# A hybrid decoder layer on one core: the router's one-hots hold two ranks side by side, ids are divided once per four heads, and a spilled tile is asked for earlier

## The chip, the core and the metric

The kernel runs on one core of a Trainium2 chip. Time is device microseconds (us) of one execution of the whole program. The engines are called PE (TensorE, matrix multiplication), DVE (VectorE), ACT (ScalarE), POOL (GpSimd) and SP (SyncE, which here only starts transfers). Each engine takes its instructions strictly in its own order, and an instruction that waits holds back everything behind it on that engine.

## What is computed

One decoder layer for 512 tokens of width 1024, in float32: RMS norm, a projection, two recurrent branches (HGRN2 and retention) that are gated and merged, and then PEER, a mixer of 16384 tiny experts, of which each token uses 128. The part that matters here is PEER:

```python
s = jnp.einsum('thpd,hpkd->thpk', q, sub_keys)      # 8 heads, 2 halves, 128 keys
top_s, top_i = lax.top_k(s, 16)
cand = top_s[:, :, 0, :, None] + top_s[:, :, 1, None, :]
cand_idx = top_i[:, :, 0, :, None] * 128 + top_i[:, :, 1, None, :]
best_s, best_c = lax.top_k(cand.reshape(T, 8, 256), 16)
expert_idx = jnp.take_along_axis(cand_idx.reshape(T, 8, 256), best_c, axis=-1)
gates = jax.nn.softmax(best_s, axis=-1)
...
act = gelu(einsum('td,thkd->thk', x, expert_u[expert_idx]))
out = einsum('thk,thkd->td', gates * act, expert_v[expert_idx])
```

After it a residual sum and a final RMS norm give the output.

## The kernel before

A float32 product is made of three float32r matmuls: each operand is split into a high part, which ACT rounds (L76), and a low part, which DVE subtracts (L77); `mm3` (L89 to L92) multiplies low by high, high by high and high by low. Every 1 MB block of weights is loaded by SP into one of three `raw` buffers (L81), split by ACT and DVE into one of three `w` buffers, and used by PE; the third matmul of a group, L92 where the block stands on the left, is the one that needs DVE's low part.

The program runs in stages. Projections and the two branches come first (to about 856 us). Then come three stages that interleave two kinds of work. PE multiplies the first 384 tokens with all 16384 rows of expert_u and later of expert_v, since nearly every expert is used by some token; the last 128 tokens are done on DVE alone, from table rows that POOL gathers by index (`gather_step`, L674 to L689, four `row` buffers). The first 88 of 128 groups of 128 experts of expert_u are multiplied ahead (`u_ahead`, L698), between the router's and the gate stage's other work; their results go to DRAM (`spill`).

The **router** (L804 to L818) takes the eight heads one after the other. For a head, `route_keys` is PE's query projection; `route_top` (twice) finds the 16 best keys of each half on DVE; `route_pick` (L760 to L802), called Pick below, sums the candidates, finds the 16 best, and turns their positions into expert ids. For this it compares the positions with a table of 50 or 20 candidate numbers (`oh`, a one-hot in float16, L791), multiplies by the candidates' ids (`pr`, L794) and sums (`ef`, L795). The first 8 ranks need only 20 candidates, the last 8 need 50; four token tiles times 8 ranks make 640 and 1600 elements a row. Four small instructions (L798 to L801) divide an id into the two key numbers, and L802 writes those of the last 128 tokens to `e_last`, by which POOL gathers. Between these stand three blocks of expert_u per head, five at the last (`U_R`; a block holds two groups), and up to six gathered rows.

The **gate stage** (L862 to L890) makes, for 12 blocks of 32 tokens, a matrix of 128 x 128 gates a token: DVE builds float16 one-hots of eight tokens a step (`oa`, `ob`, L869, L870) and scales them (`og`), PE multiplies them (L881), ACT copies them to `stage` (L884), and ACT's queue writes `stage` to DRAM (`gd`, L890). `U_G` says after which of the steps a block is multiplied ahead.

The **V stage** (L900 on) multiplies the last 40 groups of expert_u (kind "new"), reads the spilled results back (kind "old", L955), multiplies by the gates (`gt`, read from `gd`, L906; L916), splits (w_hi, w_lo, L917) and multiplies with expert_v into six sums in PSUM (L928). At its first blocks PE's results lie in two PSUM buffers, which ACT empties (L635).

Then `finish` (L651 to L672) adds each tile's sum, normalises and writes out; of the four tiles the last 128 tokens come first, and tile 2 (`tt == DT - 1`) comes last. `rsqrt_mean` (L100 to L114) is the norms' helper: ACT's square root, DVE's reciprocal and one Newton step.

The order on each engine isn't the program's order. A scheduler places the instructions by their readiness in its own model and by priority; `fetch` (L601) gives the loads and splits of a block 30 places of priority (`PRIO`), so that they are placed ahead of work that the program has earlier. `order` (L584 to L598) lists the blocks: numbers 0 to 51 are multiplied ahead or belong to the router, and block 52 is the first of the V stage.

Of the kernel before, what the change touches and what calls it, by code (L numbers as in the profile page):

```python
# [20 lines left out]
D = 1024  # L21
# [23 lines left out]
U_R, U_G = ((2,) * 8, (1,) * 7 + (3,)), (0, 1, 0, 1, 0, 1, 0, 0)  # L45
GATHER_END = 4
PRIO = 30
G_SCALE = 2.0 ** 15
# [4 lines left out]
def block_kernel(ctx, tc, a, out):  # L53
# [46 lines left out]
    def rsqrt_mean(ss, k, n, name):  # L100

        v = small.tile([128, k], F32, name=name + "v", tag=f"rs_v{k}")
        DVE.tensor_scalar(v, ss, 1.0 / n, EPS, op0=OP.mult, op1=OP.add)
        s = small.tile([128, k], F32, name=name + "s", tag=f"rs_s{k}")
        ACT.activation(s, v, AF.Sqrt)
        r = small.tile([128, k], F32, name=name + "r", tag=f"rs_r{k}")
        DVE.reciprocal(r, s)
        t = small.tile([128, k], F32, name=name + "t", tag=f"rs_t{k}")
        DVE.tensor_tensor(t, r, r, op=OP.mult)
        DVE.tensor_tensor(t, t, v, op=OP.mult)  # L110
        DVE.tensor_scalar(t, t, -0.5, 1.5, op0=OP.mult, op1=OP.add)
        r2 = small.tile([128, k], F32, name=name + "q", tag=f"rs_q{k}")
        DVE.tensor_tensor(r2, r, t, op=OP.mult)
        return r2  # L114
# [486 lines left out]
    def fetch():  # L601
        if len(blocks) == len(order):
            return
        kind, pr = order[len(blocks)]
        with tc.high_priority(offset=PRIO):
            fetch_block(kind, pr)
# [44 lines left out]
    def finish(tt):  # L651
# [7 lines left out]
        for nb in range(2):  # L659
# [4 lines left out]
            ACT.activation(junk[:, n], d, AF.Square, accum_out=ss[:, nb:nb + 1])  # L664
        st = small.tile([128, 1], F32, name="fst", tag="ss1")
# [3 lines left out]
        for nb in range(2):  # L669
            n = slice(nb * 512, (nb + 1) * 512)  # L670
            DVE.scalar_tensor_tensor(res[:, n], acc[:, tt, n], r, wrow[:, n], op0=OP.mult, op1=OP.mult)
            nc.sync.dma_start(out[tt * 128:(tt + 1) * 128, n], res[:, n])  # L672
# [36 lines left out]
    with tc.tile_pool(name="rout", bufs=1, reuse_waits="tile") as ro:  # L709
# [8 lines left out]
        iotac = ro.tile([128, NCAND + NCAND8], F16, name="iotac")  # L718
        DVE.tensor_copy(iotac, iotaf)
        best = ro.tile([128, TT, PH, TOPK], F32, name="best")  # L720
        ids_a = ro.tile([128, TT, PH, TOPK], F32, name="ids_a")
# [38 lines left out]
        def route_pick(state, hd):  # L760
# [5 lines left out]
            def sums(dst, src, widths, offs):  # L766
                ones = sum(w == 1 for w in widths)
                n = len(widths) - ones
                lead = list(dst.shape[:-1])
                for i in range(n):  # L770
                    w = widths[i]
                    DVE.tensor_tensor(dst[..., offs[i]:offs[i] + w],
                                      src(0)[..., i:i + 1].to_broadcast(lead + [w]),
                                      src(1)[..., :w], op=OP.add)
                DVE.tensor_tensor(dst[..., offs[n]:offs[n] + ones], src(0)[..., n:n + ones],
                                  src(1)[..., 0:1].to_broadcast(lead + [ones]), op=OP.add)
# [8 lines left out]
            posh = ro.tile([128, TT, TOPK], F16, name="posh", tag="posh")  # L785
            DVE.tensor_copy(posh, pos)
            ef = ro.tile([128, TT, TOPK], F32, name="ef", tag="ef")
            for lo, n, io, ids in ((0, NCAND8, iotac[:, NCAND:], cid8), (8, NCAND, iotac[:, :NCAND], cand[:, 1])):
                shape = [128, TT, 8, n]
                oh = ro.tile(shape, F16, name="oh", tag=f"oh{n}")  # L790
                DVE.tensor_tensor(oh, io[:, None, None, :].to_broadcast(shape),  # L791
                                  posh[:, :, lo:lo + 8, None].to_broadcast(shape), op=OP.is_equal)
                pr = ro.tile(shape, F32, name="pr", tag=f"pr{n}")
                DVE.tensor_tensor(pr, oh, ids[:, :, None, :].to_broadcast(shape), op=OP.mult)  # L794
                DVE.tensor_reduce(ef[:, :, lo:lo + 8], pr, axis=X, op=OP.add)  # L795
            posf = ro.tile([128, TT, TOPK], F32, name="posf", tag="posf")
            af = ids_a[:, :, hd, :]
            DVE.tensor_scalar(posf, ef, 1.0 / NK, -63.5 / NK, op0=OP.mult, op1=OP.add)  # L798
            DVE.tensor_scalar(posf, posf, 12582912.0, None, op0=OP.add)
            DVE.tensor_scalar(af, posf, 12582912.0, None, op0=OP.subtract)  # L800
            DVE.scalar_tensor_tensor(ids_b[:, :, hd, :], af, -float(NK), ef, op0=OP.mult, op1=OP.add)  # L801
            DVE.tensor_copy(e_last[:, hd * TOPK:(hd + 1) * TOPK], ef[:, TT - 1, :])  # L802
# [97 lines left out]
    with tc.tile_pool(name="vp", bufs=2, reuse_waits="tile") as vp:  # L900
# [9 lines left out]
        def v_group(g, acts, gt, w_hi, w_lo):  # L910
            todo = []
            for pr in range(GE // 2):
                hi, lo = take("v", g * GE // 2 + pr)
                two = slice(2 * pr, 2 * pr + 2)
                w = acts[:, two, :].rearrange("p e (b t) -> p e b t", t=GT)
                DVE.tensor_tensor(w, w, gt[:, :, two, :].rearrange("p b e t -> p e b t"), op=OP.mult)  # L916
                split(w_hi[:, two, :], w_lo[:, two, :], acts[:, two, :])  # L917
# [26 lines left out]
        acts = {groups[0][1]: new_acts()}  # L944
        gates = {vs[0]: load_gates(vs[0])}
        for kind, g in groups:
            if kind != "v" and g not in acts:
# [6 lines left out]
            if kind == "old":  # L954
                nc.sync.dma_start(acts[g].rearrange("p e t -> p (e t)"), spill[g])  # L955
# [84 lines left out]
```

## Time and profile before

| what | us |
|---|---|
| median of three runs (2112.39 to 2117.42) | 2114.75 |
| the profiled execution | 2116.79 |
| its span, first to last instruction | 2115.0 |
| PE busy in the span | 2074.8 |
| DVE busy | 1501.1 |
| ACT busy | 809.0 |
| mean granted PE clock | 0.995 |

Times in the profile count from the span's start. Busy time of PE overlaps: a matmul starts before the one ahead of it has ended, so the sum of single durations is more than the time they took. An entry such as "PE mm L92 <- DVE w L77: 14.8, 9, 3.3" says that PE stood idle ahead of L92's matmuls for 14.8 us in 9 places, the longest 3.3 us, until DVE's L77 had written `w`. "L77 DVE ... x37 | 84.4, 2282" is a group of 37 instructions, busy 84.4 us in all, 2282 ns each.

### The profile page before, as it was taken

How to read it: one execution, taken by the hardware profiler on the slowest of the kernel's cores; microseconds unless marked ns; L12 is line 12 of the kernel's file. 1: busy time of each engine (PE TensorE's matmuls, PEld its weight loads, DVE VectorE, ACT ScalarE, POOL GpSimd, SP SyncE). 2: the span in 40 equal slices, each digit the busy share in tenths (PEclk: the TensorE clock that was granted, in tenths of full speed). 3: DMA queues.
4: the chain of work that ended last, by engine and by line, in shares of the span. 5: the costliest groups of instructions: out<-in, count | busy, mean ns of one | idle time of the engine just before them, and what ended most of it. 6: DMA issues, size and time to landing. Idle time of an engine off the chain costs nothing.

```text
span 2115.0 us, 27164 instructions
## 1 busy us (share of the span) xinstructions
PE 2074.8 (98%) x10635; PEld 1803.0 (85%) x10635; DVE 1501.1 (71%) x2847; ACT 809.0 (38%) x959; POOL 401.3 (19%) x271
## 2 busy tenths in 40 slices
PE   9999999999999999999989999999999999999998
PEld 6888888888888788899888999988888888888876
DVE  4677674454345445599899899987877887787776
ACT  4344342244233523333322377763323333233332
POOL 0000000000000000021311211123444443554450
PEclk9999999999999999999999999999999999999999
DMA  5212112322232232365565678899989999989993
GB/s 193 80 63 71 67 60 95 105 80 85 80 104 81 90 139 80 127 229 197 207 216 195 235 273 318 329 339 363 350 325 339 339 352 340 330 326 351 334 335 125
DMA packets 139490, 441.33 MB, mean 209 GB/s; under 512 B 9825, under 2 KB 59105, under 8 KB 120418
## 3 DMA queue, kind: packets, MB, share of 16 engines
q1 hardware_dynamic: 94288, 261.85, 35.6%
q0 software_dynamic: 37008, 135.28, 17.2%
q10 hardware_dynamic: 8066, 42.48, 5.2%
q8 instruction: 83, 1.36, 0.3%
q14 instruction: 45, 0.37, 0.0%
HBM read 395.00 MB, written 44.56 MB: 208 GB/s over the span
## 4 chain that ended last, share of the span: by engine, by line
PE 76%; DVE 13%; issue 4%; DMA 4%; ACT 2%; POOL 1%; SPq 0%; DVEq 0%; ACTq 0%; POOLq 0%
PE mm L90 16%; PE mm L92 16%; PE mm L91 16%; PE sum L92 7%; PE sum L90 7%; PE sum L91 7%; DVE w L77 3%; DMA row<-in_expert_v_dram,e_last 2%; DMA row<-in_expert_u_rows_dram,e_last 2%; PE aux L881 1%; PE aux L334 1%; DVE scr L727 1%; PE aux L376 1%; PE aux L470 1%; DVE idx L729 1%
## 5 line engine op out<-in xcount | busy, mean ns | idle before, releaser
L77 DVE TENSOR_TENSOR w<-raw,w 128x2048 fp32r<-128x2048 f32 x198 | 452.6, 2287 | 237.2 <-ACT w L76 236.5
L92 PE MATMUL mm<-h_hi,w 128*128 128x384 f32 (+1 forms) x1536 | 547.9, 357 | 17.0 <-DVE w L77 14.8
L90 PE MATMUL mm<-h_lo,w 128*128 128x384 f32 (+1 forms) x1536 | 551.0, 359 | 2.8 <-ACT acts L635 2.4
L91 PE MATMUL mm<-h_hi,w 128*128 128x384 f32 (+1 forms) x1536 | 547.8, 357 | 0.0
L76 ACT ACTIVATE w<-raw 128x2048 fp32r<-128x2048 f32 x198 | 378.8, 1913 | 416.6 <-PE mm L92 204.8
L92 PEld LDWEIGHTS mm<-h_hi,w 128*128 128x128 f32 x1536 | 291.4, 190 | 39.8 <-DVE w L77 17.9
L90 PEld LDWEIGHTS mm<-h_lo,w 128*128 128x128 f32 x1536 | 291.5, 190 | 23.2 <-ACT acts L635 2.7
L91 PEld LDWEIGHTS mm<-h_hi,w 128*128 128x128 f32 x1536 | 291.5, 190 | 19.3
L90 PE MATMUL sum<-w,w_hi 128*128 128x512 f32 x768 | 299.0, 389 | 2.5 <-DVE w L77 2.5
L92 PE MATMUL sum<-w,w_lo 128*128 128x512 f32 x768 | 299.0, 389 | 1.7 <-DVE w_lo L77 1.7
L91 PE MATMUL sum<-w,w_hi 128*128 128x512 f32 x768 | 298.9, 389 | 0.0
L645 POOL DMA_INDIRECT row<-in_expert_u_rows_dram,e_last x128 | 181.1, 1414 | 566.6 <-DVE junk L679 340.9
L645 POOL DMA_INDIRECT row<-in_expert_v_dram,e_last x128 | 216.8, 1694 | 241.3 <-DVE acc L686 213.6
L686 DVE SCALAR_TENSOR_TENSOR acc<-row,dots,acc 128x1024 f32<-128x1024 f32 x128 | 164.0, 1281 | 35.3 <-DMA row<-in_expert_v_dram,e_last 33.7
L679 DVE SCALAR_TENSOR_TENSOR junk<-row,h_last 128x1024 f32<-128x1024 f32 x128 | 156.3, 1221 | 34.2 <-DMA row<-in_expert_u_rows_dram,e_last 33.5
L90 PEld LDWEIGHTS sum<-w,w_hi 128*128 128x128 f32 x768 | 144.2, 188 | 33.0 <-DVE w L77 3.4
L92 PEld LDWEIGHTS sum<-w,w_lo 128*128 128x128 f32 x768 | 144.2, 188 | 32.0 <-DVE w_lo L77 2.1
L91 PEld LDWEIGHTS sum<-w,w_hi 128*128 128x128 f32 x768 | 144.2, 188 | 29.7
L711 POOL DMA_DIRECT2D keys<-in_keys_dram x1 | 0.7, 714 | 859.6 <-DVE acc L571 859.6
L90 PE MATMUL mm<-w,h_hi 128*128 128x512 f32 x384 | 151.2, 394 | 0.0
L92 PE MATMUL mm<-w,h_lo 128*128 128x512 f32 x384 | 150.4, 392 | 0.0
L91 PE MATMUL mm<-w,h_hi 128*128 128x512 f32 x384 | 150.4, 392 | 0.0
(270 smaller groups left out, 2455.8 us busy)
## 6 DMA issues: line engine op xcount, KB each, us to landing
raw<-in_expert_u_dram SPq DMA_DIRECT2D x64, 1024.0 KB
raw<-in_expert_v_dram SPq DMA_DIRECT2D x64, 1024.0 KB
gd<-stage ACTq DMA_DIRECT2D x12, 2048.0 KB
gt<-gd SPq DMA_DIRECT2D x32, 768.0 KB
spill<-actw ACTq DMA_DIRECT2D x44, 384.0 KB
acts<-spill SPq DMA_DIRECT2D x22, 768.0 KB
raw<-in_w_rv_dram SPq DMA_DIRECT2D x8, 1024.0 KB
raw<-in_w_rg_dram SPq DMA_DIRECT2D x8, 1024.0 KB
```

The costliest lines, as they stand in the source:

```text
L76: ACT.activation(hi, src, AF.Copy)
L77: DVE.tensor_tensor(lo, src, hi.bitcast(F32), op=OP.subtract)
L90: PE.matmul(ps, lhi, rlo, start=first, stop=False)
L91: PE.matmul(ps, lhi, rhi, start=False, stop=False)
L92: PE.matmul(ps, llo, rhi, start=False, stop=last)
L334: PE.matmul(ps[:, c * 192:(c + 1) * 192], k[:, (c0 + c) * 128:(c0 + c + 1) * 128], mv[:, c0 + c, :, :].rearrange("p v t -> p (v t)"), star ...
L376: PE.matmul(po[:, j * 128:(j + 1) * 128], amat(i, j), v[:, i, hd * 128:(hd + 1) * 128], start=(i == 0), stop=(i == j))
L470: PE.matmul(ps[:, :w], k[e][:, i * 128:(i + 1) * 128], q[e][:, i * 128:], start=(e == 0), stop=(e == 1))
L645: POOL.indirect_dma_start(out=r, out_offset=None, in_=src, in_offset=bass.IndirectOffsetOnAxis(ap=e_last[:, i:i + 1], axis=0))
L679: tc.keep_in_program_order(DVE.scalar_tensor_tensor(junk, r, 1.0, h_last, op0=OP.mult, op1=OP.mult, accum_out=dots[:, i:i + 1]))
L686: tc.keep_in_program_order(DVE.scalar_tensor_tensor(x_last, r, dots[:, i - 128:i - 127], x_last, op0=OP.mult, op1=OP.add))
L727: DVE.match_replace(scratch, vals[:, 0:8], src, -3e38)
```

## The change

**Pick.** The table of candidate numbers holds each number twice, and `oh` gets the shape [16, n, 2]: two neighbouring ranks lie side by side in the last dimension, so every operand of the comparison has step 1 there. The product and the sum are made for each of the two ranks by itself, so two instructions become four (twice), of half the size. The ids stay in a tile for all heads, and the division into key numbers is done after heads 3 and 7, for four heads at a time. In `sums`, candidate rows of equal width go into one instruction, which takes one instruction of 16 elements off each head.

**Priorities and places.** `U_G` spaces the blocks of the gate stage otherwise. Block 0 gets 180 places of priority instead of 30, blocks 54 and 55 none. The first spilled tile is asked for before the V stage's loop, ahead of the gates (`gt`) and so of the table rows that the loop asks for, and in the first group of expert_v the products with the gates and their high parts are kept in program order, ahead of the loads of expert_v.

**Norms and the end.** `rsqrt_mean` takes two DVE instructions less for one column (one less for four). In `finish` the second half of each tile goes out by ACT's queue; for tile 2 the product with the norm's weights is made before the root is known, and the two halves of the last multiplication run on DVE and ACT.

```diff
--- before.py
+++ after.py
-U_R, U_G = ((2,) * 8, (1,) * 7 + (3,)), (0, 1, 0, 1, 0, 1, 0, 0)
+U_R, U_G = ((2,) * 8, (1,) * 7 + (3,)), (0, 1, 0, 0, 1, 0, 1, 0)
 GATHER_END = 4
 PRIO = 30
+OWN = AHEAD // 2 + 8
...
-        DVE.tensor_scalar(v, ss, 1.0 / n, EPS, op0=OP.mult, op1=OP.add)
+        DVE.tensor_scalar(v, ss, -0.5 / n, -0.5 * EPS, op0=OP.mult, op1=OP.add)
         s = small.tile([128, k], F32, name=name + "s", tag=f"rs_s{k}")
-        ACT.activation(s, v, AF.Sqrt)
+        ACT.activation(s, v, AF.Sqrt, scale=-2.0)
         r = small.tile([128, k], F32, name=name + "r", tag=f"rs_r{k}")
         DVE.reciprocal(r, s)
         t = small.tile([128, k], F32, name=name + "t", tag=f"rs_t{k}")
-        DVE.tensor_tensor(t, r, r, op=OP.mult)
-        DVE.tensor_tensor(t, t, v, op=OP.mult)
-        DVE.tensor_scalar(t, t, -0.5, 1.5, op0=OP.mult, op1=OP.add)
+        if k == 1:
+            DVE.scalar_tensor_tensor(t, r, v, r, op0=OP.mult, op1=OP.mult)
+        else:
+            DVE.tensor_tensor(t, r, r, op=OP.mult)
+            DVE.tensor_tensor(t, t, v, op=OP.mult)
         r2 = small.tile([128, k], F32, name=name + "q", tag=f"rs_q{k}")
-        DVE.tensor_tensor(r2, r, t, op=OP.mult)
+        DVE.scalar_tensor_tensor(r2, t, 1.5, r, op0=OP.add, op1=OP.mult)
...
     def fetch():
-        if len(blocks) == len(order):
+        n = len(blocks)
+        if n == len(order):
             return
-        kind, pr = order[len(blocks)]
-        with tc.high_priority(offset=PRIO):
+        if n in (OWN + 2, OWN + 3):
+            fetch_block(*order[n])
+            return
+        with tc.high_priority(offset=PRIO if n else 6 * PRIO):
+            fetch_block(*order[n])
 
...
+        if tt == DT - 1:
+            scaled = rowp.tile([128, D], F32, name="scaled", tag="row")
+            for nb in range(2):
+                n = slice(nb * 512, (nb + 1) * 512)
+                DVE.tensor_tensor(scaled[:, n], acc[:, tt, n], wrow[:, n], op=OP.mult)
...
-            DVE.scalar_tensor_tensor(res[:, n], acc[:, tt, n], r, wrow[:, n], op0=OP.mult, op1=OP.mult)
-            nc.sync.dma_start(out[tt * 128:(tt + 1) * 128, n], res[:, n])
+            if tt < DT - 1 or tt == TT - 1:
+                DVE.scalar_tensor_tensor(res[:, n], acc[:, tt, n], r, wrow[:, n], op0=OP.mult, op1=OP.mult)
+            elif nb == 0:
+                DVE.tensor_scalar(res[:, n], scaled[:, n], r, None, op0=OP.mult)
+            else:
+                ACT.activation(res[:, n], scaled[:, n], AF.Copy, scale=r)
+            (nc.sync if nb == 0 else nc.scalar).dma_start(out[tt * 128:(tt + 1) * 128, n], res[:, n])
...
-        iotac = ro.tile([128, NCAND + NCAND8], F16, name="iotac")
-        DVE.tensor_copy(iotac, iotaf)
+        iotac = ro.tile([128, NCAND + NCAND8, 2], F16, name="iotac")
+        DVE.tensor_copy(iotac, iotaf[:, :, None].to_broadcast([128, NCAND + NCAND8, 2]))
...
-            posh = ro.tile([128, TT, TOPK], F16, name="posh", tag="posh")
-            DVE.tensor_copy(posh, pos)
-            ef = ro.tile([128, TT, TOPK], F32, name="ef", tag="ef")
-            for lo, n, io, ids in ((0, NCAND8, iotac[:, NCAND:], cid8), (8, NCAND, iotac[:, :NCAND], cand[:, 1])):
-                shape = [128, TT, 8, n]
+            posh = ro.tile([128, 2, TT, 8], F16, name="posh", tag="posh")
+            DVE.tensor_copy(posh.rearrange("p h c k -> p c h k"), pos.rearrange("p c (h k) -> p c h k", h=2))
+            for half, n, io, cid in ((0, NCAND8, iotac[:, NCAND:], cid8), (1, NCAND, iotac[:, :NCAND], cand[:, 1])):
+                shape = [128, TT * 4, n, 2]
                 oh = ro.tile(shape, F16, name="oh", tag=f"oh{n}")
-                DVE.tensor_tensor(oh, io[:, None, None, :].to_broadcast(shape),
-                                  posh[:, :, lo:lo + 8, None].to_broadcast(shape), op=OP.is_equal)
-                pr = ro.tile(shape, F32, name="pr", tag=f"pr{n}")
-                DVE.tensor_tensor(pr, oh, ids[:, :, None, :].to_broadcast(shape), op=OP.mult)
-                DVE.tensor_reduce(ef[:, :, lo:lo + 8], pr, axis=X, op=OP.add)
-            posf = ro.tile([128, TT, TOPK], F32, name="posf", tag="posf")
-            af = ids_a[:, :, hd, :]
-            DVE.tensor_scalar(posf, ef, 1.0 / NK, -63.5 / NK, op0=OP.mult, op1=OP.add)
-            DVE.tensor_scalar(posf, posf, 12582912.0, None, op0=OP.add)
-            DVE.tensor_scalar(af, posf, 12582912.0, None, op0=OP.subtract)
-            DVE.scalar_tensor_tensor(ids_b[:, :, hd, :], af, -float(NK), ef, op0=OP.mult, op1=OP.add)
-            DVE.tensor_copy(e_last[:, hd * TOPK:(hd + 1) * TOPK], ef[:, TT - 1, :])
+                two = posh[:, half].rearrange("p c (u two) -> p (c u) two", two=2)
+                DVE.tensor_tensor(oh, io[:, None, :, :].to_broadcast(shape),
+                                  two[:, :, None, :].to_broadcast(shape), op=OP.is_equal)
+                pr = ro.tile([128, 2, TT * 4, n], F32, name="pr", tag=f"pr{n}")
+                shape = [128, TT, 4, n]
+                for two in range(2):
+                    prt = pr[:, two].rearrange("p (c u) n -> p c u n", c=TT)
+                    DVE.tensor_tensor(prt, oh[:, :, :, two].rearrange("p (c u) n -> p c u n", c=TT),
+                                      cid[:, :, None, :].to_broadcast(shape), op=OP.mult)
+                    DVE.tensor_reduce(ids[:, :, hd, 8 * half + two:8 * half + 8:2], prt, axis=X, op=OP.add)
+            DVE.tensor_copy(e_last[:, hd * TOPK:(hd + 1) * TOPK], ids[:, TT - 1, hd, :])
+            if hd % 4 == 3:
+                e, af, bf = (x[:, :, hd - 3:hd + 1, :].rearrange("p c h k -> p c (h k)") for x in (ids, ids_a, ids_b))
+                posf = ro.tile([128, TT, 4 * TOPK], F32, name="posf", tag="posf")
+                DVE.tensor_scalar(posf, e, 1.0 / NK, -63.5 / NK, op0=OP.mult, op1=OP.add)
+                DVE.tensor_scalar(posf, posf, 12582912.0, None, op0=OP.add)
+                DVE.tensor_scalar(af, posf, 12582912.0, None, op0=OP.subtract)
+                DVE.scalar_tensor_tensor(bf, af, -float(NK), e, op0=OP.mult, op1=OP.add)
...
-                hi, lo = take("v", g * GE // 2 + pr)
                 two = slice(2 * pr, 2 * pr + 2)
                 w = acts[:, two, :].rearrange("p e (b t) -> p e b t", t=GT)
-                DVE.tensor_tensor(w, w, gt[:, :, two, :].rearrange("p b e t -> p e b t"), op=OP.mult)
-                split(w_hi[:, two, :], w_lo[:, two, :], acts[:, two, :])
+                pin = tc.keep_in_program_order if count[0] < GE else lambda x: x
+                pin(DVE.tensor_tensor(w, w, gt[:, :, two, :].rearrange("p b e t -> p e b t"), op=OP.mult))
+                pin(ACT.activation(w_hi[:, two, :], acts[:, two, :], AF.Copy))
+                DVE.tensor_tensor(w_lo[:, two, :], acts[:, two, :], w_hi[:, two, :].bitcast(F32), op=OP.subtract)
+                hi, lo = take("v", g * GE // 2 + pr)
...
+        def old_acts(g):
+            acts[g] = new_acts()
+            nc.sync.dma_start(acts[g].rearrange("p e t -> p (e t)"), spill[g])
+        old_acts(next(g for kind, g in groups if kind == "old"))
         gates = {vs[0]: load_gates(vs[0])}
         for kind, g in groups:
-            if kind != "v" and g not in acts:
+            if kind == "new" and g not in acts:
                 acts[g] = new_acts()
             if kind == "new":
                 for pr in range(GE // 2):
                     u_pair(g * GE // 2 + pr, lambda j: acts[g][:, 2 * pr + j, :])
                     pace(2)
                 continue
-            if kind == "old":
-                nc.sync.dma_start(acts[g].rearrange("p e t -> p (e t)"), spill[g])
+            if kind == "old" and g not in acts:
+                old_acts(g)
             n = vs.index(g) + 1
             if n < len(vs):
                 gates[vs[n]] = load_gates(vs[n])
```

The first place is DVE in the router, at Pick of one head (here the fifth before and the sixth after); `oh`, `pr` and `ef` or `ids` are the one-hots, products and ids, `w` is a block's low part. Before:

```order
L786 CAST posh<-pos 128x64
L791 TENSOR_TENSOR oh<-iotac,posh 128x640
L791 TENSOR_TENSOR oh<-iotac,posh 128x1600
L794 TENSOR_TENSOR pr<-oh,cid_8080 128x640
L794 TENSOR_TENSOR pr<-oh,cand 128x1600
L795 TENSOR_REDUCE ef<-pr 128x4x8 x2
L77 TENSOR_TENSOR w<-raw,w 128x2048
L798 TENSOR_SCALAR posf<-ef 128x64
L802 CAST e_last<-ef 128x16
```

And now on the same engine:

```order
L808 CAST posh<-pos 128x4x2x8
L813 TENSOR_TENSOR oh<-iotac,posh 128x640
L813 TENSOR_TENSOR oh<-iotac,posh 128x1600
L78 TENSOR_TENSOR w<-raw,w 128x2048
L819 TENSOR_TENSOR pr<-oh,cid_8386 128x320 x2
L821 TENSOR_REDUCE ids<-pr 128x4x4 x2
L819 TENSOR_TENSOR pr<-oh,cand 128x800 x2
L821 TENSOR_REDUCE ids<-pr 128x4x4 x2
L822 CAST e_last<-ids 128x16
```

The comparison keeps its size and its two instructions, product and sum become eight instructions of half the size, the division is gone from this head, and the block's low part stands a few rows earlier.

The second place is SP's queue where the V stage begins: the last blocks of expert_u, the first of expert_v, the gates and the spilled tile. Before:

```order
L81 DMA raw<-in_expert_u_dram 128x2048 x29
L81 DMA raw<-in_expert_v_dram 128x2x1024 x2
L906 DMA gt<-gd 128x12x128 x2
L81 DMA raw<-in_expert_v_dram 128x2x1024
L955 DMA acts<-spill 128x1536
```

And now:

```order
L82 DMA raw<-in_expert_u_dram 128x2048 x29
L82 DMA raw<-in_expert_v_dram 128x2x1024 x2
L978 DMA acts<-spill 128x1536
L933 DMA gt<-gd 128x12x128
L82 DMA raw<-in_expert_v_dram 128x2x1024
```

The spilled tile moved past two loads of gates and one block of expert_v.

The third place is ACT at the same seam: the copies of the last gates (`stage`), the high parts of blocks 53 to 56 (`w`) and the results of PE's first V-stage blocks (`acts`). Before:

```order
L884 ACTIVATE stage<-aux 128x4x128 x7
L76 ACTIVATE w<-raw 128x2048
L890 DMA gd<-stage 128x4096
L76 ACTIVATE w<-raw 128x2048
L635 ACTIVATE acts<-mm 128x384 x4
L76 ACTIVATE w<-raw 128x2048
```

And now:

```order
L911 ACTIVATE stage<-aux 128x4x128 x2
L77 ACTIVATE w<-raw 128x2048
L917 DMA gd<-stage 128x4096
L77 ACTIVATE w<-raw 128x2048
L642 ACTIVATE acts<-mm 128x384 x4
L77 ACTIVATE w<-raw 128x2048
```

The high part of block 55 (the second `w` row) stands ahead of the four `acts` rows in both, although its priority is gone; only one of the earlier high parts moved up between the copies.

More of the change, by code (lines that the diff above doesn't have):

```diff
@@ L601, in fetch @@
     def fetch():
-        if len(blocks) == len(order):
+        n = len(blocks)
+        if n == len(order):
             return
-        kind, pr = order[len(blocks)]
-        with tc.high_priority(offset=PRIO):
-            fetch_block(kind, pr)
+        if n in (OWN + 2, OWN + 3):
[3 more added lines that the diff above has]
+            fetch_block(*order[n])
     def fetch_block(kind, pr):
@@ L717, in block_kernel @@
                       channel_multiplier=0, allow_small_or_imprecise_dtypes=True)
-        iotac = ro.tile([128, NCAND + NCAND8], F16, name="iotac")
-        DVE.tensor_copy(iotac, iotaf)
+        iotac = ro.tile([128, NCAND + NCAND8, 2], F16, name="iotac")
+        DVE.tensor_copy(iotac, iotaf[:, :, None].to_broadcast([128, NCAND + NCAND8, 2]))
         best = ro.tile([128, TT, PH, TOPK], F32, name="best")
+        ids = ro.tile([128, TT, PH, TOPK], F32, name="ids")
         ids_a = ro.tile([128, TT, PH, TOPK], F32, name="ids_a")
@@ L766, in sums @@
             def sums(dst, src, widths, offs):
-                ones = sum(w == 1 for w in widths)
-                n = len(widths) - ones
                 lead = list(dst.shape[:-1])
[L770 to L776, printed above, removed]
+                lo = 0
+                while lo < len(widths):
+                    w = widths[lo]
+                    n = sum(x == w for x in widths) if w == 1 or len(lead) == 2 else 1
+                    shape = lead + [n, w] if n > 1 and w > 1 else lead + [n * w]
+                    d, x, y = dst[..., offs[lo]:offs[lo] + n * w], src(0)[..., lo:lo + n], src(1)[..., :w]
+                    if n > 1 and w > 1:
+                        d = d.rearrange("p c (n w) -> p c n w", n=n)
+                        x, y = x[..., :, None], y[..., None, :]
+                    DVE.tensor_tensor(d, x.to_broadcast(shape), y.to_broadcast(shape), op=OP.add)
+                    lo += n
             sums(cand, lambda p: top[:, :, p], WIDTHS, OFFS)
```

## Prediction

> **What bounds the kernel now.** I read the profiled execution by stages first (busy time in windows), then PE's waits, then the rows around single waits, and the groups by shape last. The page and its windows (length, then busy us and count for PE, PEld, DVE, ACT and POOL, then granted clock, DMA share and GB/s):
>
> ```profile
> span 2115.0 us, 27164 instructions
> ...
> 0.00:856.00 856.00, 849.99 (x3947) 695.90 (x3948) 457.29 (x951) 322.33 (x470) 0.20 (x4) 1.00 0.26 91
> 1000.00:1216.00 216.00, 201.25 (x1074) 190.30 (x1073) 195.52 (x676) 65.99 (x74) 45.35 (x32) 0.97 0.61 214
> 1216.00:1403.00 187.00, 186.15 (x1531) 180.60 (x1530) 176.55 (x250) 133.19 (x142) 24.83 (x23) 1.00 0.85 309
> 1403.00:1450.00 47.00, 41.39 (x266) 39.91 (x266) 30.19 (x38) 22.32 (x24) 16.16 (x11) 0.96 1.02 359
> 1450.00:2040.00 590.00, 590.00 (x2783) 511.32 (x2782) 463.74 (x406) 194.08 (x162) 276.13 (x168) 1.00 0.94 341
> ```
>
> PE is the bound nearly everywhere: 850 of 856 us up to the router, 186 of 187 in the gate stage, all 590 in most of the V stage. Nothing that lightens another engine there can bring time. It is open in three places: the router from 1000 us on (PE idle 14.8 of 216 us), the seam at 1403 to 1450 (5.6 of 47), and the end. PE's waits name what it waited for, and when; the first two rows are the window 856 to 1216, the next three 1216 to 1500, then 1500 to the end, then the whole span:
>
> ```profile
> PE mm L92 <- DVE w L77: 14.8, 9, 3.3
> PE mm L92 <- DVE nv L103: 2.3, 1, 2.3
> ...
> PE mm L90 <- ACT acts L635: 2.4, 1, 2.4
> PE sum L92 <- DVE w_lo L77: 1.7, 1, 1.7
> PE aux L881 <- DVE og L874: 1.2, 2, 0.8
> ...
> PE sum L90 <- DVE w L77: 2.5, 2, 1.6
> ...
> PE aux L136 <- DVE xn L130: 2.1, 3, 1.6
> PE aux L496 <- DVE ron L493: 0.9, 5, 0.2
> ```
>
> A long wait costs more than itself. These windows follow the second of the router's waits, its last one over 2 us, the wait for `acts` and the wait for `w_lo`:
>
> ```profile
> 1064.60:1067.80 3.20, 3.20 (x12) 3.20 (x11) 3.10 (x30) 0.00 (x0) 0.00 (x0) 0.50 1.04 379
> ...
> 1180.60:1183.90 3.30, 3.28 (x10) 3.29 (x11) 3.30 (x26) 0.00 (x0) 1.71 (x2) 0.50 0.76 246
> 1419.60:1422.80 3.20, 3.12 (x10) 3.12 (x11) 0.81 (x1) 0.41 (x2) 0.00 (x0) 0.50 1.02 413
> 1448.60:1452.00 3.40, 3.40 (x15) 2.82 (x16) 2.40 (x4) 0.20 (x1) 0.94 (x1) 1.00 1.06 290
> ```
>
> After the longer waits the granted clock is 0.50 for about 3.4 us, so PE loses some 1.7 us more; after the 1.7 us wait it stays at 1.00. Four of the router's nine waits were followed by it: PE lost there 14.8 + 4 x 1.7 = 21.6 us.
>
> What makes `w` late is seen in the order of time, on DVE and PE (the bracket is the idle time ahead):
>
> ```profile
> 1059.78 1.23 DVE L679 SCALAR_TENSOR_TENSOR junk<-row,h_last 128x1024 f32<-128x1024 f32 x1 [5.71 <-DMA row<-in_expert_u_rows_dram,e_last]
> 1061.88 2.28 DVE L77 TENSOR_TENSOR w<-raw,w 128x2048 fp32r<-128x2048 f32 x1
> ...
> 1064.22 0.48 PE L92 MATMUL mm<-h_hi,w 128*128 128x384 f32 x1 [2.07 <-DVE w L77]
> ...
> 1067.91 2.56 DVE L791 TENSOR_TENSOR oh<-iotac,posh 128x640 f16<-128x640 f16 x2
> ```
>
> DVE works without a pause (195.5 of 216 us), and what pause there is, is a table row that hasn't landed:
>
> ```profile
> DVE junk L679 <- DMA row<-in_expert_u_rows_dram,e_last: 13.6, 7, 5.7
> ```
>
> That row is the only one of DVE's waits between 890 and 1200 us. DVE never waits for PE there, so from the first stall on the router is as long as DVE's own list plus these waits, and PE takes what it is given.
>
> **The change part by part.** *Pick.* DVE's groups by shape (mean ns behind the busy time); the last three are other stages' instructions that resemble the new ones:
>
> ```profile
> L791 DVE TENSOR_TENSOR oh<-iotac,posh 128x1600 f16<-128x1600 f16 x8 | 14.6, 1819 | 0.0
> L791 DVE TENSOR_TENSOR oh<-iotac,posh 128x640 f16<-128x640 f16 x8 | 6.6, 822 | 0.2
> L801 DVE SCALAR_TENSOR_TENSOR ids_b<-ids_a,ef 128x64 f32<-128x64 f32 x8 | 1.7, 210 | 0.0
> L798 DVE TENSOR_SCALAR posf<-ef 128x64 f32<-128x64 f32 x8 | 1.5, 185 | 0.1
> ...
> L869 DVE TENSOR_TENSOR oa<-iot,a_t 128x1024 f16<-128x1024 f16 x48 | 32.3, 686 | 0.0
> L405 DVE TENSOR_SCALAR k<-f 128x512 f32<-128x512 f32 x8 | 3.4, 427 | 0.5
> L290 DVE TENSOR_TENSOR Fn<-f 128x256 f32<-128x256 f32 x8 | 3.4, 419 | 0.0
> ```
>
> The two `oh` rows give (1819 - 822) / 960 = 1.04 ns an element and 157 ns fixed. `oa` is the same comparison in the layout that `oh` gets, 1024 elements in 686 ns: less the 157 fixed, 0.52 ns an element. So 1600 elements take 982 ns and 640 take 487: 1.17 us saved per head. Against it, four instructions more. Each has the fixed 157, but the two `oh` in the order of time end after 2.56 us where their durations add to 2.64, so a follower starts 80 ns before the one ahead ends: 4 x 77 = 0.31 us. The division: four instructions of 64 elements (3 x 185 + 210, less 4 x 80: 0.44 us a head) become four of 256 for four heads; between 185 at 64 and 427 at 512 a TENSOR_SCALAR of 256 takes 289, and the last 157 + 266 = 423; together 0.97 us, 0.24 a head: 0.20 saved. One small instruction less in the candidate sums: 0.08. In all -1.17 + 0.31 - 0.20 - 0.08 = -1.14 us a head, -9.1 us for eight heads, all on DVE's list and so on the path. If the four instructions cost their full 157 ns, it is -6.5. The waits for table rows (13.6 us) stay about as they are, since rows five and six are asked for when rows one and two have been used, which moves with DVE; I allow 4 us to either side. **Router: -9.1 (-13 to -2.5).** What is late next is the same low part, behind a shorter Pick.
>
> [...]
>
> *The seam at the V stage.* ACT, DVE and SP there:
>
> ```profile
> 1417.34 1.91 ACT L76 ACTIVATE w<-raw 128x2048 fp32r<-128x2048 f32 x1 [4.36 <-PE mm L92]
> ...
> 1443.54 1.83 DVE L916 TENSOR_TENSOR acts<-acts,gt 128x768 f32<-128x768 f32 x2 [5.47 <-DMA acts<-spill]
> ...
> 1403.06 12.65 SPq L81 DMA_DIRECT2D raw<-in_expert_v_dram  x2
> 1420.73 4.11 SPq L906 DMA_DIRECT2D gt<-gd  x2
> 1429.24 0.40 SPq L955 DMA_DIRECT2D acts<-spill  x1
> ```
>
> The spilled tile was issued at 1429.2 and used at 1443.5, 14.3 us later. Now it stands right behind the second block of expert_v (issued by 1415.7), so with the same 14.3 us it is there at 1430. The gates are asked for behind it; they wait for the last write of `gd`, so 1420.7 stays, and with 14.3 us they are there at 1435, well before PE reaches its first sum at 1446. **The 1.7 us wait goes: -1.7 (-1.7 to 0).** What would be late next is ACT's w_hi, which now stands behind a block's high part; its cover is the matmuls of block 55.
>
> The 2.4 us wait for `acts` I leave: ACT's `w` at 1417.34 waited for PE to finish block 52, whose buffer it takes, and PE's results of block 52 wait behind it for 1.91 + 0.5 us. ACT's order is the same in the changed program, so wait and slow clock stay (**0; -4.1 if ACT were free**). On DVE at 860 us I also find the order unchanged: acc, then `w`, so the 2.3 us (row "nv") stay. In the gate stage one step fewer trails behind the last block multiplied ahead: of PE's 1.2 us for `og` and 0.4 for `ob` about half goes: **-0.8 (-1.6 to +1)**. Of the 2.5 us late in the V stage I take **-1.0 (-2.5 to +2)**, since the gates are asked for a block earlier near the end, and a wait for table rows also stands there.
>
> *Norms and end.* The chain that ended last, and DVE's and ACT's work there:
>
> ```profile
> 2110.13 0.17 DVE ft L111
> 2110.32 0.17 DVE fq L113
> ...
> 2110.51 1.41 DVE L671 SCALAR_TENSOR_TENSOR res<-acc,fq,h_last 128x512 f32<-128x512 f32 x2
> ...
> L664 ACT ACTIVATE junk<-acc 128x512 f32<-128x512 f32 x6 | 3.8, 632 | 18.4 <-DVE acc L663 18.4
> ```
>
> Steps of the chain are 0.19 us apart, and two go: -0.4. Then 1.41 us of two halves one after the other become the longer of DVE's half (427 by L405) and ACT's (632 by L664): -0.7. The product `scaled` is covered by the wait for the last sum and by ACT's square; without that cover it costs up to 0.7. ACT's new transfers wait for DVE's second half ahead of the next tile's square, which has half a us to spare. **End: -1.1 (-1.5 to +0.5).** The shorter norms reach PE where it waited for `xn` and `ron` (2.1 and 0.9 us in eight places), at most 0.4 each; the scheduler gives part back by placing the transposes sooner: **-0.8 (-1.8 to +1)**. Elsewhere PE's own work hides them.
>
> Sum: -9.1 - 1.7 - 0.8 - 1.0 - 1.1 - 0.8 = **-14.5 us**. The profiled execution took 2116.8 us, its span and 1.8 us around it; so it would come to 2102.3. It lies 2.0 us above the median of the three runs, 2114.75, from which I go: **2100 us**.
>
> **The rivals.** *PE covered altogether.* If the relief falls where the waits are, all nine go and with them the slow clock: 21.6 instead of 9.1, which gives 2114.75 - 27.0 = 2088. For it: DVE and PE are within a tenth of each other in the router. Against: DVE's list stays the longer by more than it loses. [...]
>
> *Table rows take it.* DVE comes to its rows sooner, and they land when they did: the 1.1 us a head turn into waiting. One row waited 5.7 us already. Then only 5.4 us are left: 2109.
>
> *The comparison isn't faster.* If `oh` keeps 1819 ns in its new shape, the router gains nothing: 2109 too. `oa` speaks against it.
>
> *Slower: `pr` reads every second element.* The products now read `oh`, float16, with step 2, which no row shows for float16. At half the rate, 2240 elements a head would take 2.33 us more, the router 8 x (2.33 - 1.14) = 9.5 us more, and the kernel 2114.75 - 5.4 + 9.5 = 2119. From 0.5 ns more an element on, the router loses. Against it: `Fn` reads float32 with step 2, and its 419 ns are what 256 elements at step 1 would take.
>
> **How the numbers follow.** My forecast 0.68, from 2093 to 2108; PE covered 0.08; table rows 0.11; comparison not faster 0.03; slower 0.06; the rest, a worse order somewhere in the unchanged stages, 0.04. Adding the lower half of the first rival and the 2109 to 2112 of the next two gives 2089 to 2112. A measurement of this kernel tells about 0.2%, 4.2 us, from no change. Faster by more: the forecast, the first rival and half of the next two: 0.82. Slower: 0.06, mostly the strided read; within: 0.12.
>
> **What would show it.** The two `oh` near 980 and 490 ns, `pr` near 990 and 490; DVE's heads about 1.1 us shorter; PE's wait for `w` in the router near 6 to 9 us, still with some windows of clock 0.50; no wait for `w_lo` at the first sum, but still 2.4 us for `acts`; the end 1 us shorter after PE's last matmul. I am wrong if `pr` is longer than 1.2 us, if DVE's waits for rows grow by what Pick lost, or if PE waits in the stages where it never did.

## The result and the profile after

The changed kernel takes 2103.33 us (median of 5 runs, 2101.18 to 2107.57), the kernel before 2113.92 us (5 runs): ratio 0.995, 95% interval 0.9933 to 0.9966. Two later measurements of it gave 0.996 (0.9945 to 0.9976) and 0.9949 (0.9935 to 0.9962); over all its 16 runs the median is 2103.5. The forecast was 2100.

The two profiled executions lie at opposite ends of their kernels' runs (2116.8 and 2101.2), so they differ by 15.6 us where the medians differ by 10.6. The page of the changed kernel, and its windows for the same two stretches as before (length, then busy us and count for PE, PEld, DVE, ACT and POOL, then granted clock, DMA share and GB/s):

```profile
span 2099.4 us, 27112 instructions
...
1000.00:1216.00 216.00, 208.48 (x1192) 199.20 (x1191) 197.34 (x666) 76.11 (x87) 42.95 (x32) 0.98 0.62 216
...
1403.00:1450.00 47.00, 42.89 (x215) 39.81 (x216) 30.71 (x37) 14.33 (x17) 16.10 (x13) 0.96 1.01 367
```

In the router's window PE's idle time fell from 14.8 to 7.5 of 216 us (it now holds some 10 us of the gate stage). The window 1403 to 1450 shows 4.1 of 47 us idle, but the stages come some 13 us earlier now, so it cuts off one wait and part of another. PE's waits say more, first in the window 856 to 1216, then in 1216 to 1500; from 1500 on there is none:

```profile
PE mm L93 <- DVE w L78: 8.1, 5, 2.6
PE mm L93 <- DVE nv L104: 2.3, 1, 2.3
...
PE sum L91 <- ACT w_hi L945: 3.2, 1, 3.2
PE mm L91 <- ACT acts L642: 2.4, 1, 2.4
PE sum L93 <- DVE w_lo L946: 1.7, 1, 1.7
PE aux L908 <- DVE og L901: 1.0, 4, 0.4
PE aux L908 <- DVE ob L897: 0.4, 1, 0.4
```

The wait for `w` went from 14.8 to 8.1 us, `nv` and `acts` stayed as forecast. At the seam a wait of 3.2 us for `w_hi` is new, and a wait of 1.7 us for `w_lo` is there as before, only at the second group now, 18.8 us behind the first sum. DVE's groups in the router, and its waits from 890 to 1200 us:

```profile
L819 DVE TENSOR_TENSOR pr<-oh,cand 128x800 f32<-128x800 f16 x16 | 15.1, 982 | 0.0
L813 DVE TENSOR_TENSOR oh<-iotac,posh 128x1600 f16<-128x1600 f16 x8 | 7.9, 984 | 0.0
L819 DVE TENSOR_TENSOR pr<-oh,cid 128x320 f32<-128x320 f16 x16 | 7.1, 484 | 0.0
L813 DVE TENSOR_TENSOR oh<-iotac,posh 128x640 f16<-128x640 f16 x8 | 3.9, 489 | 0.2
L829 DVE SCALAR_TENSOR_TENSOR ids_b<-ids_a,ids 128x256 f32<-128x256 f32 x2 | 0.8, 419 | 0.0
L826 DVE TENSOR_SCALAR posf<-ids 128x256 f32<-128x256 f32 x2 | 0.6, 284 | 0.0
...
DVE junk L697 <- DMA row<-in_expert_u_rows_dram,e_last: 12.0, 8, 2.7
DVE w L78 <- ACT w L77: 4.7, 1, 4.7
```

Every duration came as worked out: `oh` 984 and 489 ns (982 and 487), `pr` 982 and 484 (990 and 490), so the products pay nothing for reading every second float16. The rows cost 12.0 us after 13.6; they did not take what Pick gave. (The last row is a wait at the router's end; the kernel before has it too, at 1210 us.)

To compare executions I cut them where PE's waits mark the same place: the first low part in the router (end of the wait for `nv`), the end of the wait for `acts`, the first sum of the V stage, PE's last matmul. All in us; the last column is the time at which the clock first reached 1.00:

| profiled execution | to the router's low part | on to `acts` | on to the first sum | on to PE's end | tail | span | clock |
|---|---|---|---|---|---|---|---|
| before | 862.7 | 557.0 | 26.5 | 661.1 | 7.7 | 2115.0 | 13.2 |
| changed | 858.0 | 545.9 | 30.0 | 658.4 | 7.1 | 2099.4 | 5.7 |
| changed, second profile | 860.4 | 543.0 | 28.4 | 662.2 | 7.1 | 2101.1 | 13.4 |
| Pick alone | 862.6 | 547.0 | 26.7 | 658.3 | 7.7 | 2102.1 | 13.8 |
| old Pick, the rest changed | 857.8 | 557.3 | 30.0 | 659.0 | 7.1 | 2111.2 | 5.8 |
| Pick, norms, end | 860.3 | 545.8 | 26.7 | 659.9 | 7.1 | 2099.7 | 13.7 |
| fastest version | 858.2 | 546.8 | 26.6 | 658.3 | 7.1 | 2097.0 | 6.0 |

### The profile page after: what moved, and what is told of

It is laid out like the page before. It is cut to its first block, busy times and chain, and to the rows that moved or that the text cites. A ratio compares the mean times of both kernels' runs of the same rounds, so it can differ in the third digit from the quotient of the medians.

```text
span 2099.4 us, 27112 instructions
## 1 busy us (share of the span) xinstructions
PE 2066.9 (98%) x10635; PEld 1797.8 (86%) x10635; DVE 1482.8 (71%) x2784; ACT 811.0 (39%) x960; POOL 390.7 (19%) x271
## 4 chain that ended last, share of the span: by engine, by line
PE 79%; DVE 15%; DMA 3%; issue 2%; ACT 1%; SPq 0%; POOL 0%; DVEq 0%; ACTq 0%
PE mm L91 16%; PE mm L93 16%; PE mm L92 16%; PE sum L93 8%; PE sum L92 8%; PE sum L91 8%; DVE w L78 3%; DMA row<-in_expert_u_rows_dram,e_last 2%; PE aux L908 1%; PE aux L337 1%; DVE og L901 1%; DVE scr L747 1%; DVE junk L697 1%; DVE ids L821 1%; PE aux L379 1%
## 5 line engine op out<-in xcount | busy, mean ns | idle before, releaser
L93 PE MATMUL mm<-h_hi,w 128*128 128x384 f32 (+1 forms) x1536 | 546.8, 356 | 10.4 <-DVE w L78 8.1
L92 PE MATMUL mm<-h_hi,w 128*128 128x384 f32 (+1 forms) x1536 | 547.0, 356 | 0.0
L92 PEld LDWEIGHTS mm<-h_hi,w 128*128 128x128 f32 x1536 | 290.5, 189 | 19.5
L652 POOL DMA_INDIRECT row<-in_expert_u_rows_dram,e_last x128 | 170.3, 1330 | 580.1 <-DVE junk L697 359.7
L91 PEld LDWEIGHTS sum<-w,w_hi 128*128 128x128 f32 x768 | 144.2, 188 | 33.1 <-ACT w_hi L945 3.5
```

What stands on the lines that cost most here:

```text
L91: PE.matmul(ps, lhi, rlo, start=first, stop=False)
L92: PE.matmul(ps, lhi, rhi, start=False, stop=False)
L93: PE.matmul(ps, llo, rhi, start=False, stop=last)
L652: POOL.indirect_dma_start(out=r, out_offset=None, in_=src, in_offset=bass.IndirectOffsetOnAxis(ap=e_last[:, i:i + 1], axis=0))
```

## The experiments

The theory after the result: Pick's shorter list on DVE makes the gain, in the router; the new order at the V seam costs. Its rivals: the other edits made the gain and the rows take Pick's; or the seam's new wait is a matter of one execution.

### The changed kernel again

Edit: none.

> The changed kernel once more, beside the other runs of this call, with a second profile. Theory (Pick's shorter list on DVE gives nearly all of it): 2101 to 2106 us, 9 to 12 us under the kernel before. The profiles also differ at the start: the granted clock reached 1.00 at 13.2 us in the kernel before and at 5.7 us here. If the order of the work sets that, it is 5.7 us again; if it falls by chance, some other time.

Measured: 2104.19 us, ratio 0.996 (0.9945 to 0.9976). The granted clock reached 1.00 at 13.4 us this time, so the start falls by chance; it is worth 2.3 us (858.0 and 860.4 in the table). The order of work doesn't set it: it is the same in both. PE's matmuls at the start, of the first and then of the second profile of the same kernel:

```profile
5.30 2.13 PE L183 MATMUL aux<-one_row,ones 1*128 1x512 f32 x4
...
5.31 3.78 PE L183 MATMUL aux<-one_row,ones 1*128 1x512 f32 x4
```

### The old Pick in the changed kernel, the new one in the kernel before

Edits, in short: the parts of the diff that touch `iotac`, `ids`, `sums` and Pick are taken back, or are made alone. In both, PE, ACT and SP have exactly the order of the kernel that they come from.

```diff
-    oh = ro.tile([128, TT * 4, n, 2], F16, name="oh", tag=f"oh{n}")
+    oh = ro.tile([128, TT, 8, n], F16, name="oh", tag=f"oh{n}")
...
-    if hd % 4 == 3:
+    DVE.tensor_scalar(posf, ef, 1.0 / NK, -63.5 / NK, op0=OP.mult, op1=OP.add)
```

> The changed kernel with the old Pick; PE, ACT and SP keep their order to the last instruction. Theory: the router is as long as DVE's list, so about 10 us come back: 2113 us (2110 to 2117), PE's waits for w in the router 13 to 16 us in place of 8.1, four stretches of clock 0.50 there in place of two. Rival (the table rows take what Pick gives, and the other edits made the gain): 2102 to 2107, waits of PE for w as in the changed kernel, DVE's waits for rows some 8 us shorter.

> The kernel before with the new Pick alone; PE, ACT and SP keep their order. Theory: 2104 us (2101 to 2107), 10 us under the kernel before, PE's waits for w in the router near 8 us. Rival (the other edits made the gain): 2110 to 2114.

Measured: with the old Pick 2116.01 us, 1.0012 of the kernel before (1.0002 to 1.0022), a little slower than it; with the new Pick alone 2103.84, 0.9948 (0.9935 to 0.9962), as fast as the whole change. PE's waits in the router, of the first and then of the second run:

```profile
PE mm L93 <- DVE w L78: 15.5, 9, 4.8
...
PE mm L92 <- DVE w L77: 7.4, 4, 2.7
```

The theory holds: Pick is worth 10 to 12.5 us, all of it between the router's start and `acts` (557.0 against 547.0 in the table). All the other edits together are worth nothing, or cost up to 2 us.

### Each comparison made twice

Each `oh` is written twice with the same result; only DVE's order changes.

```diff
+                for _ in range(2):
-                DVE.tensor_tensor(oh, io[:, None, :, :].to_broadcast(shape),
-                                  two[:, :, None, :].to_broadcast(shape), op=OP.is_equal)
+                    DVE.tensor_tensor(oh, io[:, None, :, :].to_broadcast(shape),
+                                      two[:, :, None, :].to_broadcast(shape), op=OP.is_equal)
```

> The changed kernel with each comparison of Pick made twice, its second result the same as its first; only DVE's order changes. It adds 984 + 489 less 2 x 80 ns a head, 10.5 us in eight heads, to DVE alone. Theory (the router is as long as DVE's list): 2114 us (2112 to 2118), PE's waits for w in the router 13 to 18 us. Rival (DVE's waits for rows or PE's own length cover it): 2104 to 2109.

Measured: 2113.67 us, 10.2 more than the changed kernel's 2103.5, for 10.5 us more on DVE. PE's waits for `w` in the router:

```profile
PE mm L93 <- DVE w L78: 18.2, 10, 3.9
```

A microsecond on DVE's list in the router is about a microsecond of the kernel, in both directions: the forecast's way of counting is right.

### The seam taken back, and the seam and the gate stage one by one

The changed kernel with the old V seam (spilled tile, `v_group` and the priorities of the two blocks there as before):

```diff
-        if n in (OWN + 2, OWN + 3):
-            fetch_block(*order[n])
-            return
...
-        old_acts(next(g for kind, g in groups if kind == "old"))
```

> The changed kernel with the old V seam (spilled tile, gates, low parts and block priorities there as before). Theory (the new order at the seam costs): PE's waits of 3.2 us for w_hi and 1.7 for w_lo go, one of 1.7 for w_lo is back, so 3 us less than the changed kernel: 2100 us (2098 to 2102). Rival (the new order gives the 1.7 us that were forecast and the 3.2 us is a matter of this one execution): 2104 to 2106.

Measured: 2108.31 us, ratio 0.9972 (0.9959 to 0.9984): 4 to 5 us slower than with the new seam, not 3 faster. My theory fell here. PE waited 7.0 us at its first sum; SP's issues of a block and of the spilled tile and DVE's product on it show why. The first three rows are this run's, the next three those of Pick alone:

```profile
1411.89 7.87 SPq L82 DMA_DIRECT2D raw<-in_expert_v_dram  x1
1419.88 1.05 SPq L978 DMA_DIRECT2D acts<-spill  x1
...
1433.09 1.83 DVE L939 TENSOR_TENSOR acts<-acts,gt 128x768 f32<-128x768 f32 x2 [11.36 <-DMA acts<-spill]
...
1413.76 3.63 SPq L81 DMA_DIRECT2D raw<-in_expert_v_dram  x1
1417.50 0.40 SPq L964 DMA_DIRECT2D acts<-spill  x1
...
1430.98 1.83 DVE L925 TENSOR_TENSOR acts<-acts,gt 128x768 f32<-128x768 f32 x2 [2.94 <-DMA acts<-spill]
```

The tile is asked for 17.2 us after the wait for `acts` (which ended at 1402.69), and its product starts 13.2 us later. With Pick alone, whose seam is the same, it was asked for 8.0 us after that wait (which ended at 1409.53), the product started 13.5 us later, and PE did not wait at all. Most of the delay lies in SP's issues ahead of the tile: 7.5 us for the gates and 7.9 for the block, against 4.1 and 3.6; why they take longer isn't shown. So the old seam isn't late by itself; something else in the changed kernel makes it late. Left to suspect: the gate stage's new list `U_G`, which decides behind which gates the last blocks are multiplied. Hence the next two, both with the old `U_G`: Pick, norms and end on the old seam, and the same on the new one.

```diff
-U_R, U_G = ((2,) * 8, (1,) * 7 + (3,)), (0, 1, 0, 0, 1, 0, 1, 0)
+U_R, U_G = ((2,) * 8, (1,) * 7 + (3,)), (0, 1, 0, 1, 0, 1, 0, 0)
```

> The kernel before with the new Pick, the shorter norms and the new end, but the old gate stage and the old V seam. Theory (norms give 2.2 us up to the first block of the router and 0.6 at the end, and Pick alone leaves no wait at the first sum): 2101 us (2099 to 2103), less than the changed kernel. Rival (what the norms give is taken back behind them): 2103 to 2106.

> The run with Pick, norms and end, and the new V seam too, but the old gate stage (U_G) and the old priority of the first block. Theory (ACT's order at the new seam, a block's high part ahead of the second half of w_hi, makes the wait): PE waits 2.5 to 3.5 us for w_hi at its first sum, 2103 to 2106 us. Rival (the new U_G, which takes multiplied blocks from behind the last gates, makes the seam late): no wait over 0.5 us at the first sum, 2099 to 2102.

Measured: 2101.5 us (0.9944, 0.9931 to 0.9956) and 2101.3 (0.9946, 0.9933 to 0.9959). The first has no wait at the first sum. The second has the 3.2 us for `w_hi` again, so ACT's order makes that wait whatever `U_G` is; but its time is the rival's, and lies 2.2 us under the changed kernel. Theory and rival each had half of it. Its waits from 1216 to 1500:

```profile
PE sum L91 <- ACT w_hi L945: 3.2, 1, 3.2
PE mm L91 <- ACT acts L642: 2.4, 1, 2.4
PE aux L908 <- DVE og L901: 1.1, 2, 0.8
PE aux L908 <- ACT stage L911: 0.9, 4, 0.2
PE aux L908 <- DVE ob L897: 0.4, 1, 0.4
```

### The first group's high and low parts earlier

ACT at the seam in the changed kernel (start, length, what; the bracket is the idle time ahead):

```profile
1429.34 0.84 ACT L945 ACTIVATE w_hi<-acts 128x768 fp32r<-128x768 f32 x1 [2.17 <-DVE acts L944]
1430.89 1.91 ACT L77 ACTIVATE w<-raw 128x2048 fp32r<-128x2048 f32 x1 [0.70 <-PE mm L93]
1432.71 0.47 ACT L642 ACTIVATE acts<-mm 128x384 f32<-128x384 f32 x1
1433.08 0.83 ACT L945 ACTIVATE w_hi<-acts 128x768 fp32r<-128x768 f32 x1
...
1433.96 0.50 PE L91 MATMUL sum<-w,w_hi 128*128 128x512 f32 x1 [3.16 <-ACT w_hi L945]
```

Between the two halves of `w_hi` stands the high part `w` of a block of expert_v. It waits until PE is done with the block whose buffer it takes, which is when PE wants its first sum; and PE starts 0.05 us after the second half, in all six profiles with this order. It is the third block of expert_v (block 58). The program fetches it behind the second half, so it stands ahead of that half by its 30 places of priority, which blocks 54 and 55 alone have lost. The edit writes both halves one block ahead:

```diff
                     u_pair(g * GE // 2 + pr, lambda j: acts[g][:, 2 * pr + j, :])
                     pace(2)
+                    if pr == 0 and g == groups[1][1]:
+                        for i in range(GE // 2):
+                            weigh(i, acts[vs[0]], *gates[vs[0]])
```

where `weigh` holds the three instructions (product, high part, low part) and `v_group` leaves them out for the first group. A first try had `count[0] == 0` in place of the group's number, which holds behind two groups:

> The changed kernel with the first group's products, high and low parts written one block earlier. Theory (ACT's order costs the wait of 3.2 us): it goes, the slow clock behind it too, and the 1.7 to 2.3 us for the second group's w_lo go or stay: 2099 us (2097 to 2102). Rival (the gates or the spilled tile land too late for it anyway, or the block's high part is late in its place): 2103 to 2106.

Measured: 2109.64 us. This run multiplies the first group's activations by their gates twice, the first time a group too early: ACT stood at `w_hi` for tile and gates, PE's results waited behind it, and PE lost 9.2 us in one wait for `acts` (11.6 with the usual one). It says nothing on the theory but that the products can come too early. With the group's number in its place, the same edit in the changed kernel and in the run with the old `U_G`:

> The changed kernel with the first group's products, high and low parts written between the last two blocks that are multiplied ahead of it, once (the run before this one wrote them behind two groups, and so a group earlier than meant and twice). Theory (ACT's order at the seam makes PE's wait of 3.2 us): PE has no wait over 0.5 us at its first sum, and 2100 us (2098 to 2102). Rival (gates or spilled tile land too late, so ACT and DVE stand waiting for them and hold up the blocks): a new wait of 2 us or more, 2103 to 2107.

> The same edit in the run with Pick, norms, end and the new seam, but the old gate stage. Theory: without its wait of 3.2 us for w_hi it takes 2098 us (2096 to 2100), less than the kernel before and the changed kernel. Rival: as for the run beside it, 2101 to 2104.

Measured: 2106.1 us (0.9962, 0.9948 to 0.9975) and 2098.71 us (0.9928, 0.9915 to 0.9942). These two differ in `U_G` alone: raising the first block's priority sixfold changes no engine's order in either. With the old `U_G` the wait at the seam is gone, and the median is 2.6 us lower. With the new one the time is the rival's; the waits at the seam are 1.8 us for `w_lo` at the first group, and 1.2 and 0.4 at the second. DVE's first product in the run with the new `U_G` and then in that with the old:

```profile
1427.25 0.96 DVE L941 TENSOR_TENSOR acts<-acts,gt 128x768 f32<-128x768 f32 x1 [9.38 <-issue]
...
1421.02 0.96 DVE L941 TENSOR_TENSOR acts<-acts,gt 128x768 f32<-128x768 f32 x1 [8.24 <-issue]
```

Both came 26 to 28 us after the last gates began to be written out (1399.44 and 1394.95), but the first sum was due 33.1 us after that write with the new `U_G` and 36.7 with the old. The new list takes 3.6 us of cover from between the last gates and the V stage.

The run with the new `U_G` shows one thing more, PE's first sum and ACT's second half:

```profile
1432.54 0.39 PE L91 MATMUL sum<-w,w_hi 128*128 128x512 f32 x1
...
1435.86 0.85 ACT L942 ACTIVATE w_hi<-acts 128x768 fp32r<-128x768 f32 x1 [4.96 <-DVE acts L941]
```

Here the sum starts 3.3 us ahead of the second half, so it doesn't need that half itself. Why PE was held for it in the changed kernel isn't shown; that the wait goes with ACT's order is. In one table for all (medians; 16 runs in the one field, 10 in another, 5 to 9 elsewhere; all have Pick, norms and end):

| | old seam | new seam | new seam, first group earlier |
|---|---|---|---|
| old `U_G` | 2101.5 | 2101.3 | 2098.8 |
| new `U_G` | 2108.3 | 2103.5 (the change) | 2106.1 |

In each column the new `U_G` is the slower one, by 2 to 7 us. In the last column not all of the 7 us can be placed at the seam: the profile with the new `U_G` also has a wait of PE of 4.3 us in the router, where a row came 4.1 us late; but the fastest version's second profile has that wait too.

### The fastest version beside the change

> The changed kernel a third time, beside the run that follows it. Theory: 2103 to 2106 us.

> The fastest of the runs so far a second time, beside the changed kernel on the same chip. Theory (the gate stage's new order costs, and ACT's order at the seam too): 2097 to 2101 us, 4 to 7 us under the changed kernel. Rival (the 5 us between them in the earlier calls were the spread of single executions): less than 2 us between them.

Measured, on one chip: 2103.26 and 2100.51 us, 2.75 apart, between what theory and rival said. Over all runs the medians are 2103.5 (16) and 2098.8 (10); the means are 4.0 apart, with 95% bounds of some 2 to either side (standard deviations of 2.7 and 2.2 us). It beats both kernels, by less than its first measurement showed.

## Why the prediction was right, and where it was not

**Router, -9.1: right.** Durations, overlap of followers and waits for rows came as worked out; Pick alone measured -10.2. The stretch of the table fell by 10.0. Two of the four slow stretches of PE's clock went with the waits. (The window of slow clock at 1064.60 follows the third of the router's waits, not the second; the count of four is right.)

**The full price of an instruction, -6.5: not seen.** Two `pr` of 982 ns take 1.88 us together, 80 ns less than their sum, like the pair that the forecast used.

**V seam, -1.7: the step that failed.** The tile came in time: it was asked for at 1402 and landed at 1418. The gates took longer than forecast, 19.5 us from the request (1405.6) and not 14.3: they landed at 1425.1, and the first product started 0.2 us behind them, still 5.5 us before PE wanted its first sum. What failed is the sentence on ACT's `w_hi`, "its cover is the matmuls of block 55". The `w` ahead of it waits for those very matmuls to end, so they cover nothing, and 1.91 + 0.47 + 0.83 us, less the overlaps, fall behind them: 3.16 us, in every profile that has the new seam with the halves apart. And the 1.7 us to be won were gone already: with Pick alone the old seam has no wait. By PE's waits the term is about +3, by the medians with the old `U_G` nothing (2101.3 against 2101.5, 5 runs each), and -1.7 by neither. Five runs each can't tell which of the two is nearer.

**Gate stage, -0.8: right in its place, wrong for the kernel.** The waits for `og`, `ob` and `stage` fell from 2.5 to 1.4 us. What I didn't ask is what the moved block had covered: the time from the last gates to the first sum. By the table of medians the new list costs 2 to 7 us. How it makes SP's issues at the old seam late stays open.

**Late V stage, -1.0: within its bounds.** The 2.5 us are gone in the changed kernel's profile; its second one and other runs with the new seam show 0 to 2.2 us there, for `w_lo`.

**Norms, -0.8: too small.** At about the same start of the clock (13.2 and 13.4 us) the stretch to the router fell from 862.7 to 860.4, 2.3 us, with the old seam and gate stage too (860.3). The five waits for `ron` (0.9 us) are gone, and those for `xn` fell from 2.1 to 1.4 us; the rest, some 0.7 us, no wait up to there accounts for.

**End, -1.1: half of it.** The tail is 7.1 in place of 7.7 us in all profiles. Two steps less gave 0.33 and the two halves side by side 0.69, as counted; but from the last half's end to the end of the span it now takes 3.5 us in place of 3.1. Here is the end of the chain of the changed kernel:

```profile
2094.73 0.23 DVE ft L111
2094.96 0.02 issue
2094.98 0.17 DVE fq L116
2095.15 0.02 issue
2095.17 0.72 ACT res L689
```

**The sum.** -14.5 was forecast, the medians moved by -10.6. Pick -10.2, norms -2.3 and end -0.6 make -13.1; `U_G` and the seam together gave 2 to 3 us back. That the time still came within 3.3 us of the forecast is partly luck: Pick and the norms gave 2.6 us more than they were counted for, and that made up for part of what the seam and the gate stage took. The rivals "rows take it", "comparison not faster" and "strided read" are refuted by the groups above; "PE covered" too: 8.1 us of waits for `w` are left.

## What to carry to other kernels

Before an instruction is counted as covered by some work, look whether the one ahead of it in its queue waits for the end of that same work: here ACT's `w` did, and PE stood for 3.16 us behind it. A change that moves work sooner must be asked what that work used to hide: two edits that each shorten a wait in their own place can meet at a seam and cost more than they bring. And take single parts of a bundled change by themselves: here one part of six made nearly all of the gain, and what the norms and the end won was about given back by the gate stage and the seam.

## What the runs showed of the hardware

**The granted clock changed on a grid of 3.41 us.** I had read from the trace of before that the clock was 0.50 after waits of 2.07 us and more, and not after one of 1.66. In the traces of the two kernels all changes of the granted clock but the first lie at whole multiples of 3.41 us from it, and the clock of 0.50 went with how long PE was idle in one such window: the ten windows with 2.07 to 2.95 us idle were each followed by one of 0.50 (six before, four in the changed kernel), and none of the others up to PE's last matmul was, the longest with 1.71 us. The changed kernel's wait of 3.16 us at the seam, its longest, left 1.62 and 1.53 us idle in two windows, and the clock stayed at 1.00. The same wait in two executions shows it too. It measures 2.46 us in the first (Pick, norms, end and new seam), where the grid cuts it in two, and 2.52 us in the second (the changed kernel), where it falls into one window. The rows are the three windows of each one's grid around it, with the granted clock third from the end:

```profile
1029.90:1033.30 3.40, 2.55 (x15) 2.12 (x13) 3.40 (x20) 1.28 (x2) 0.00 (x0) 1.00 0.00 0
1033.30:1036.70 3.40, 1.79 (x8) 1.48 (x9) 3.40 (x7) 1.01 (x1) 0.17 (x1) 1.00 0.59 159
1036.70:1040.10 3.40, 3.40 (x17) 2.81 (x16) 3.40 (x9) 0.00 (x0) 2.79 (x3) 1.00 0.90 333
```

```profile
1029.70:1033.10 3.40, 3.40 (x22) 3.40 (x21) 3.40 (x25) 0.09 (x1) 0.00 (x0) 1.00 0.31 117
1033.10:1036.50 3.40, 0.88 (x5) 0.45 (x4) 3.40 (x10) 2.29 (x2) 0.00 (x0) 1.00 0.29 116
1036.50:1039.90 3.40, 3.40 (x8) 2.71 (x9) 3.40 (x8) 0.00 (x0) 1.80 (x1) 0.50 0.70 226
```

Idle are 0.85 and 1.61 us in the first case, 2.52 in the second, and only there the next window is slow.

**This makes executions of one kernel differ.** The wait of 2.3 us for `nv` was followed by a clock of 0.50 in the changed kernel's first profile (859.1 to 862.3 us) and by 1.00 in its second (860.4 to 863.7). A window of 3.41 us at half the clock costs PE 1.7 us, by estimate, and the start costs 2.3 us or not. The three profiled executions of the changed kernel span 2099.4, 2101.1 and 2098.2 us. They have four, three and three slow stretches, and the full clock from 5.7, 13.4 and 5.6 us on, so by this count the first two would lie 1.7 and 2.3 us above the third; they lie 1.2 and 2.9 above it. So two profiles can't settle a difference of a few us. Of the runs of up to 2109.6 us there is no trace.
